# Products of probabilities and values in an attention kernel: one unbroken group per half pair, second head first

## Chip, cores and metric

The kernel runs on one core of one Trainium2 chip. The metric is the device time of one execution in microseconds (us); the time before the change is the median of three runs. The profile is of one further execution of the same program.

## What is computed

Two transformer blocks follow each other on 512 tokens of width 1024, all in 32-bit floats. The first block has an attention with 8 heads beside a convolution of 31 taps, and a feed-forward part; the second has a windowed attention with 16 query heads on 4 key heads ("GQA" below), then a latent attention with 16 heads ("MLA" below). The three attentions end in the same two steps, a softmax and the product of its probabilities with the values:

```python
def chunked_rel_attention(q, k, v, rel_bias):          # first block
    ...
    probs = jax.nn.softmax(scores, axis=-1).astype(v.dtype)
    out = jnp.einsum('bhcqk,bckhd->bcqhd', probs, vb)

def windowed_gqa(u, w_in, sink, w_out):                # GQA
    ...
        probs = jax.nn.softmax(jnp.concatenate([logits, sink_col], axis=-1), axis=-1)[..., :-1]
        return jnp.einsum('bkgqs,bskd->bqkgd', probs.astype(v_blk.dtype), v_blk)

def mla(u, w_in, q_norm, w_qb, kv_norm, w_kvb, w_out): # MLA
    ...
        probs = jax.nn.softmax(logits, axis=-1)
        return jnp.einsum('bhqs,bshd->bqhd', probs.astype(v.dtype), v)
```

A head has 64 columns of values in all three.

## The kernel before

Activations lie transposed: 128 features on the partitions, 512 tokens along the free dimension. A weight matrix comes in tiles of 128x1024 by DMA; ScalarE (ACT) copies a tile to a rounded form (`w_hi`, L83), VectorE (DVE) subtracts that from the tile (`w_lo`, L226), and each product with weights is three matmuls in float32r, high by high, high by low and low by high (`mm3`, L297 to L299). These are most of the work of TensorE (PE).

`attention` (from L537 on) is one generator for the three attentions; a `Spec` with the details of each is handed to it. It works on pairs of heads, 4 in the first block and 8 in each of the others. A pair has two halves of 256 queries (`hf`), a half has two blocks of 128 queries for each of the two heads, so four items. Per item:

- `scores`: a tile of scores in PSUM (`ps_s`; L837, L1266, L1610), softmax on DVE and ACT into a tile `P` in SBUF;
- `scale`, one step later: P is divided by its sum, on POOL (GpSimd) in GQA and MLA, on ACT in the first block (L556, L209, L212);
- `turn`, 3 or 4 steps later: P is turned by PE in pieces of 128x128 into `ps_pt` (L571, plain float32), and ACT copies the result into `PT` (L212), of which there are two buffers;
- `product`, two steps after the last turn of a half: for each block of 128 keys and each of the two heads one matmul of the head's 64 columns of values with the turned probabilities (L587, plain float32). The first head goes to partitions 0 to 63 of the PSUM tile `ps_o`, the second to partitions 64 to 127. A half has 8 such products in MLA, 6 in GQA, and 4 or 8 in the first block, 272 in all; the trace shows each as two matmul records, so 544. `ps_o` has one buffer for both halves of a pair; after the second half `Spec.out` reads it on DVE (and ACT) and frees it.

The attention alternates with a second generator that emits the weight matmuls of the same stage (`drive`). But the order in which the generators emit is not yet the order on the engines: a scheduler takes the emitted instructions, lets each engine take the ready one of the highest priority, by its own estimate of when operands are ready, and earlier emitted means higher priority. What comes out is a fixed list per engine, and on the chip each engine works through its list in order and waits where an operand is late. In the list of PE, the products of one half can therefore be broken up by turns, scores or weight matmuls. "Piece" below is a run of products with nothing else between them in that list.

Of the kernel before, what the change touches and what calls it, by code (L numbers as in the profile page):

```python
# [182 lines left out]
class Kernel:  # L183
# [353 lines left out]
    def attention(self, spec, pairs, ready, s):  # L537

        nc = self.nc
        items = [(p, hf, ii, hh) for p in range(pairs) for hf in range(2) for ii in range(2) for hh in range(2)]  # L540
        n = len(items)
        P, L, PT, O = {}, {}, {}, {}

        def scores(t):
            p, hf, ii, hh = items[t]
            i = 2 * hf + ii
            ps = self.ps("s")
            spec.qk(ps, p, hh, i)
            sb = s.tile([128, spec.width], F32, tag="P", name="P", bufs=spec.lag + 1)
            st = s.tile([128, 2], F32, tag="st", name="st", bufs=8)  # L550
            P[t] = spec.softmax(ps, sb, st, p, hh, i)
            L[t] = st

        def scale(t):
            st = L.pop(t)
            nc.vector.reciprocal(out=st[:, 0:1], in_=st[:, 1:2])  # L556
            if spec.scale_act:
                self.act(P[t], P[t], AF.Copy, scale=st[:, 0:1])
            else:
                self.ts(P[t], P[t], st[:, 0:1], 1.0, MUL, MUL, eng=nc.gpsimd)  # L560

        def turn(t):
            p, hf, ii, hh = items[t]
            i = 2 * hf + ii
            js = spec.keys(i)
            if (p, hf) not in PT:
                PT[p, hf] = s.tile([128, 2, spec.nj, 256], F32, tag="PT", name="PT", bufs=2)
            ps = self.ps("pt")
            x = P.pop(t)
            for a, j in enumerate(js):  # L570
                nc.tensor.transpose(ps[:, 128 * a:128 * a + 128], x[:, 128 * a:128 * a + 128], self.ident)  # L571
            j0 = js[0] - spec.first(hf)
            out = PT[p, hf][:, hh, j0:j0 + len(js), 128 * ii:128 * ii + 128]
            src = ps[:, :128 * len(js)].rearrange("p (a q) -> p a q", q=128)
            if spec.turn_act(t):
                self.act(out, src, AF.Copy)
            else:
                nc.vector.tensor_copy(out=out, in_=src)

        def product(p, hf):  # L580
            if hf == 0:
                O[p] = self.ps("o")
            pt = PT.pop((p, hf))
            js = spec.order(hf)
            for n_, (j, c0, c1) in enumerate(js):
                for hh in range(2):
                    nc.tensor.matmul(  # L587
                        out=O[p][64 * hh:64 * hh + 64, 256 * hf + c0:256 * hf + c1], lhsT=spec.v(p, hh, j),
                        rhs=pt[:, hh, j - spec.first(hf), c0:c1], start=(n_ == 0), stop=(n_ == len(js) - 1),
                        skip_group_check=True,  # L590
                    )
            if hf == 1:
                spec.out(p, O.pop(p))

        for t in range(n + spec.lag + 2):
            if t < n:
                while not ready(items[t][0]):
                    yield "wait"
                scores(t)
            if 0 <= t - 1 < n:  # L600
                scale(t - 1)
            yield
            late = t - spec.lag
            if 0 <= late < n:
                turn(late)
            if 0 <= late - 2 < n and items[late - 2][2:] == (1, 1):
                product(*items[late - 2][:2])
            yield
# [1126 lines left out]
```

## Time and profile before

| | |
|---|---|
| median of 3 runs | 1408.14 us (1407.62 to 1409.98) |
| the profiled execution | 1407.86 us, span of its instructions 1406.0 us |
| busy in the span | PE 1363.5 us (97%), DVE 898.7, ACT 684.4, POOL 268.3 |
| first block's attention and convolution | about 112 to 250 us of the span |
| GQA attention | about 820 to 985 us |
| MLA attention | about 1150 to 1313 us |

The profile names an instruction by line, engine, operation and tiles (`ps_o<-PT,V` is written from PT and V). A matmul's duration is the modelled time of one through the array; matmuls overlap, so what one costs is the distance from its start to the start of the next one. PEld is the load of a matmul's stationary operand, which can run beside another matmul. A "wait" is idle time of an engine, put down to the instruction that ended it.

### The profile page before, as it was taken

The numbers are of one execution on the slowest core, as the hardware profiler recorded it, in microseconds if no ns is written. First come the engines' busy times: TensorE is split into PE (matmuls) and PEld (weight loads), VectorE is DVE, ScalarE is ACT, GpSimd is POOL, SyncE is SP. The second block draws the span as 40 slices with busy tenths as digits, with TensorE's granted clock in tenths as the row PEclk, the third lists the DMA queues.
The fourth block names the chain that finished last, engine by engine and source line by source line (L and its number), as shares of the span: only waits on it lengthen the run. The fifth ranks groups of instructions, "written<-read, shape, count | busy, mean of one in ns | idle before, by whom it ended". The sixth has DMA issues, their size and how long they took to land.

```text
span 1406.0 us, 19239 instructions
## 1 busy us (share of the span) xinstructions
PE 1363.5 (97%) x6953; PEld 1078.5 (77%) x6953; DVE 898.7 (64%) x1560; ACT 684.4 (49%) x1222; POOL 268.3 (19%) x343
## 2 busy tenths in 40 slices
PE   6999999999899999999999999999999999999996
PEld 3887778788688888888887777777887876677785
DVE  6688999775777642355535555556586666665666
ACT  5247663434554432344424455656353467776543
POOL 0000001232201110011111134433123003332312
PEclk9999999999999999999999999999999999999998
DMA  8447626346425323323234442232233220111322
GB/s 338 149 134 200 191 90 217 98 152 238 152 86 166 115 72 98 120 91 105 70 95 158 128 129 84 79 90 76 87 124 110 90 87 22 46 38 38 109 94 68
DMA packets 55744, 162.99 MB, mean 116 GB/s; under 512 B 6753, under 2 KB 9185, under 8 KB 55650
## 3 DMA queue, kind: packets, MB, share of 16 engines
q1 hardware_dynamic: 55648, 161.76, 36.6%
q8 instruction: 55, 0.90, 0.3%
q14 instruction: 39, 0.32, 0.1%
q10 hardware_dynamic: 2, 0.00, 0.0%
HBM read 140.77 MB, written 6.29 MB: 105 GB/s over the span
## 4 chain that ended last, share of the span: by engine, by line
PE 85%; DVE 10%; ACT 2%; issue 2%; DMA 1%; SPq 0%; POOL 0%; DVEq 0%; ACTq 0%; POOLq 0%
PE ps_mm L297 21%; PE ps_mm L298 21%; PE ps_mm L299 21%; PE ps_o L587 5%; PE ps_pt L571 3%; PE ps_s L1610 3%; DVE w_lo L226 2%; PE ps_s L1266 2%; DVE conv L205 1%; PE ps_s L401 1%; DVE tA L202 1%; PE ps_pt L151 1%; PE ps_s L837 1%; ACT act_hi L212 1%; DVE act_lo L226 1%
## 5 line engine op out<-in xcount | busy, mean ns | idle before, releaser
L297 PE MATMUL ps_mm<-act_hi,w_hi 128*128 128x512 f32 (+1 forms) x1372 | 534.1, 391 | 5.1 <-ACT act_hi L212 3.9
L298 PE MATMUL ps_mm<-act_lo,w_hi 128*128 128x512 f32 (+1 forms) x1372 | 530.7, 387 | 1.7 <-DVE act_lo L205 1.6
L299 PE MATMUL ps_mm<-act_hi,w_lo 128*128 128x512 f32 (+1 forms) x1372 | 529.8, 387 | 2.1 <-DVE w_lo L226 2.1
L83 ACT ACTIVATE w_hi<-w_raw 128x1024 fp32r<-128x1024 f32 (+2 forms) x202 | 202.9, 1009 | 319.7 <-PE ps_mm L298 303.4
L226 DVE TENSOR_TENSOR w_lo<-w_raw,w_hi 128x1024 fp32r<-128x1024 f32 (+2 forms) x202 | 239.7, 1189 | 149.7 <-ACT w_hi L83 145.1
L297 PEld LDWEIGHTS ps_mm<-act_hi,w_hi 128*128 128x128 f32 x1372 | 258.8, 189 | 60.8 <-issue 5.4
L299 PEld LDWEIGHTS ps_mm<-act_hi,w_lo 128*128 128x128 f32 x1372 | 259.1, 189 | 55.5 <-DVE w_lo L226 3.2
L298 PEld LDWEIGHTS ps_mm<-act_lo,w_hi 128*128 128x128 f32 x1372 | 259.5, 189 | 53.2 <-DVE act_lo L205 2.1
L209 POOL TENSOR_SCALAR P<-P,st 128x512 f32<-128x512 f32 (+2 forms) x128 | 86.8, 680 | 175.2 <-DVE st L556 152.5
L212 ACT ACTIVATE PT<-ps_pt 128x512 f32<-128x512 f32 (+3 forms) x160 | 78.4, 497 | 32.6 <-PE ps_pt L571 31.1
L212 ACT ACTIVATE P<-P,st 128x385 f32<-128x385 f32 (+5 forms) x128 | 70.3, 557 | 49.1 <-DVE st L1279 38.7
L141 POOL TENSOR_TENSOR acc<-acc,sq 128x512 f32<-128x512 f32 x35 | 53.8, 1538 | 202.1 <-ACT sq L212 192.2
L205 DVE SCALAR_TENSOR_TENSOR conv<-u,vecs,conv 128x512 f32<-128x512 f32 x120 | 90.2, 758 | 1.0
L571 PE MATMUL ps_pt<-ident,P 128*128 128x128 f32 x496 | 83.2, 275 | 2.8 <-ACT P L212 1.7
L1066 POOL TENSOR_TENSOR val<-val,gate 128x512 f32<-128x512 f32 x22 | 28.9, 1315 | 289.3 <-ACT gate L212 289.3
L571 PEld LDWEIGHTS ps_pt<-ident,P 128*128 128x128 f32 x496 | 61.6, 140 | 25.3 <-POOL P L209 3.9
L587 PE MATMUL ps_o<-PT,V 128*64 128x256 f32 (+1 forms) x544 | 78.9, 372 | 0.5 <-ACT PT L212 0.2
L1615 DVE TENSOR_REDUCE st<-ps_s 128x1 f32<-128x512 f32 x64 | 44.0, 688 | 30.2 <-PE ps_s L1610 26.3
L1610 PE MATMUL ps_s<-Km,Qm 128*128 128x512 f32 x192 | 62.2, 425 | 0.0
L587 PEld LDWEIGHTS ps_o<-PT,V 128*64 128x64 f32 x544 | 39.0, 136 | 29.7 <-issue 15.2
L212 ACT ACTIVATE P<-ps_s,st 128x512 f32<-128x512 f32 x64 | 43.9, 686 | 20.6 <-DVE st L1615 17.1
L483 DVE CUSTOM_DVE_ANT_0 w_raw<-w_raw,c,vecs 128x1024 f32<-128x1024 f32 x32 | 44.5, 1389 | 12.9 <-DMA w_raw<-in_w_ada_dram 12.9
(254 smaller groups left out, 1643.9 us busy)
## 6 DMA issues: line engine op xcount, KB each, us to landing
w_raw<-in_w_up_dram SPq DMA_DIRECT2D x44, 512.0 KB, 3.4
w_raw<-in_w_in_dram SPq DMA_DIRECT2D x32, 512.0 KB, 4.3
w_raw<-in_w_ada_dram SPq DMA_DIRECT2D x32, 512.0 KB, 3.5
w_raw<-in_a_w_in_dram SPq DMA_DIRECT2D x18, 512.0 KB, 3.5
ada<-in_w_ada_dram SPq DMA_DIRECT2D x16, 512.0 KB, 7.1
w_raw<-in_ple_w_gate_dram SPq DMA_DIRECT2D x16, 512.0 KB, 3.3
w_raw<-in_b_w_in_dram SPq DMA_DIRECT2D x14, 512.0 KB, 3.4
Q<-stage SPq DMA_DIRECT2D x48, 128.0 KB, 2.4
```

Source lines behind the costliest of these rows:

```text
L83: k.nc.scalar.activation(out=hi, in_=src, func=AF.Copy)
L141: k.nc.gpsimd.tensor_tensor(out=self.sum, in0=self.sum, in1=x, op=ADD)
L205: return self.fix(self.nc.vector.scalar_tensor_tensor(out=out, in0=a, scalar=s, in1=b, op0=op0, op1=op1))
L209: return self.fix((eng or self.nc.vector).tensor_scalar(out=out, in0=a, scalar1=s1, scalar2=s2, op0=op0, **kw))
L212: return self.fix(self.nc.scalar.activation(out=out, in_=a, func=func, **kw))
L226: self.fix((eng or self.nc.vector).tensor_tensor(out=out, in0=x, in1=hi.bitcast(F32), op=SUB))
L297: mm(out=ps, lhsT=w[0], rhs=x[0], start=first, stop=False, **kw)
L298: mm(out=ps, lhsT=w[0], rhs=x[1], start=False, stop=False, **kw)
L299: mm(out=ps, lhsT=w[1], rhs=x[0], start=False, stop=last, **kw)
L571: nc.tensor.transpose(ps[:, 128 * a:128 * a + 128], x[:, 128 * a:128 * a + 128], self.ident)
L587: nc.tensor.matmul(out=O[p][64 * hh:64 * hh + 64, 256 * hf + c0:256 * hf + c1], lhsT=spec.v(p, hh, j), rhs=pt[:, hh, j - spec.first(hf), c ...
L1610: nc.tensor.matmul(out=ps, lhsT=Qb[p % 2][:, qa, hh, 128 * i:128 * i + 128], rhs=Kb[p % 2][:, ka, hh], start=(a == 0), stop=(a == 2))
```

## The change

The loop of the products stands inside a block of raised scheduling priority, and the two heads are emitted in the order second, first. Nothing else is changed; the same 272 products are computed.

```diff
             js = spec.order(hf)
-            for n_, (j, c0, c1) in enumerate(js):
-                for hh in range(2):
-                    nc.tensor.matmul(
...
+
+            with self.tc.high_priority():
+                for n_, (j, c0, c1) in enumerate(js):
+                    for hh in (1, 0):
+                        nc.tensor.matmul(
...
             if hf == 1:
                 spec.out(p, O.pop(p))
```

Every line of the kernel behind it has a number higher by two: L1610 becomes L1612, L1266 becomes L1268, the product L587 becomes L589.

The list of PE in MLA, where the second half of the second pair is computed, before (L571 turns, L587 products, L1610 scores, L297 and L298 weights; x8 is eight in a row):

```order
L571 MATMUL ps_pt<-ident,P 128x128
L587 MATMUL ps_o<-PT,V 64x256
L1610 MATMUL ps_s<-Km_8998,Qm_8996 128x512
L297 MATMUL ps_mm<-act_hi,w_hi 128x512
L587 MATMUL ps_o<-PT,V 64x256
L1610 MATMUL ps_s<-Km_8998,Qm_8996 128x512 x2
L587 MATMUL ps_o<-PT,V 64x256
L1610 MATMUL ps_s<-Km_8998,Qm_8996 128x512
L587 MATMUL ps_o<-PT,V 64x256 x2
L1610 MATMUL ps_s<-Km_8998,Qm_8996 128x512 x3
L587 MATMUL ps_o<-PT,V 64x256 x2
L571 MATMUL ps_pt<-ident,P 128x128
```

and with the change:

```order
L571 MATMUL ps_pt<-ident,P 128x128 x3
L1612 MATMUL ps_s<-Km_8998,Qm_8996 128x512
L571 MATMUL ps_pt<-ident,P 128x128 x3
L297 MATMUL ps_mm<-act_hi,w_hi 128x512
L1612 MATMUL ps_s<-Km_8998,Qm_8996 128x512 x2
L298 MATMUL ps_mm<-act_lo,w_hi 128x512
L589 MATMUL ps_o<-PT,V 64x256 x8
L1612 MATMUL ps_s<-Km_8998,Qm_8996 128x512 x4
```

The eight products stood in six pieces (the last, a single one, 14 matmuls further on) and stand in one now, four matmuls behind the last turn of their half.

The list of PE in GQA, where the second half of the second pair is computed, before (L1266 scores):

```order
L571 MATMUL ps_pt<-ident,P 128x128 x4
L587 MATMUL ps_o<-PT,V 64x256 x2
L1266 MATMUL ps_s<-Kg,Q 128x384 x2
L587 MATMUL ps_o<-PT,V 64x256
L1266 MATMUL ps_s<-Kg,Q 128x384 x2
L571 MATMUL ps_pt<-ident,P 128x128 x2
L587 MATMUL ps_o<-PT,V 64x256
L587 MATMUL ps_o<-PT,V 64x128 x2
L297 MATMUL ps_mm<-act_hi,w_hi 128x512
```

and with the change:

```order
L1268 MATMUL ps_s<-Kg,Q 128x384 x2
L298 MATMUL ps_mm<-act_lo,w_hi 128x512
L299 MATMUL ps_mm<-act_hi,w_lo 128x512
L297 MATMUL ps_mm<-act_hi,w_hi 128x512
L298 MATMUL ps_mm<-act_lo,w_hi 128x512
L571 MATMUL ps_pt<-ident,P 128x128 x2
L589 MATMUL ps_o<-PT,V 64x256 x4
L589 MATMUL ps_o<-PT,V 64x128 x2
L1268 MATMUL ps_s<-Kg,Q 128x384 x2
```

Three pieces became one, behind two turns that belong to the next half; the last turn of its own half lies 8 matmuls back.

Counted over the whole list, the products stand in 74 pieces before and in 40 now, one for each half: 14 and 8 in the first block, 25 and 16 in GQA, 35 and 16 in MLA. Of the 74, 42 hold an odd number of products (12, 10 and 20), in 4 of these the odd one being of 128 columns; of the 40 none does. At least 23 of the 40 stand five matmuls or fewer behind the last turn of their half. The list of the DMA queue is the same; on DVE, ACT and POOL neighbouring instructions change places.

## Rows read from the trace of the kernel before

**Rows 1.** Page, busy us (share of the span) and instructions of each engine.
```profile
PE 1363.5 (97%) x6953; PEld 1078.5 (77%) x6953; DVE 898.7 (64%) x1560; ACT 684.4 (49%) x1222; POOL 268.3 (19%) x343
```

**Rows 2.** Windows: length, then busy us of each engine, in the three attentions.
```profile
core 0: us, PE busy (x) PEld busy (x) DVE busy (x) ACT busy (x) POOL busy (x), PEclk, DMA share, GB/s
112.00:250.00 138.00, 134.45 (x678) 104.35 (x677) 129.17 (x255) 83.10 (x179) 8.19 (x10) 1.00 0.59 173
820.00:985.00 165.00, 164.41 (x902) 127.80 (x901) 98.03 (x256) 98.89 (x238) 67.16 (x138) 1.00 0.31 90
1150.00:1313.00 163.00, 161.58 (x890) 113.25 (x889) 101.60 (x198) 113.11 (x244) 52.23 (x67) 1.00 0.15 43
```

**Rows 3.** Waits of PE, whole span: us in total, times, longest.
```profile
PE ps_pt L151 <- DVE tA L202: 1.8, 1, 1.8
PE ps_pt L571 <- ACT P L212: 1.7, 1, 1.7
...
PE ps_o L587 <- ACT PT L212: 0.2, 1, 0.2
```

**Rows 4.** Timeline of PE in MLA: start us, duration, instructions merged.
```profile
1165.66 1.94 PE L587 MATMUL ps_o<-PT,V 128*64 128x256 f32 x14
1167.53 0.98 PE L1610 MATMUL ps_s<-Km,Qm 128*128 128x512 f32 x3
...
1172.84 1.95 PE L587 MATMUL ps_o<-PT,V 128*64 128x256 f32 x16
1174.72 0.97 PE L1610 MATMUL ps_s<-Km,Qm 128*128 128x512 f32 x3
...
1178.74 0.40 PE L299 MATMUL ps_mm<-act_hi,w_lo 128*128 128x512 f32 x1
1178.97 0.39 PE L297 MATMUL ps_mm<-act_hi,w_hi 128*128 128x512 f32 x1
...
1185.69 0.50 PE L1610 MATMUL ps_s<-Km,Qm 128*128 128x512 f32 x1
1186.03 0.40 PE L297 MATMUL ps_mm<-act_hi,w_hi 128*128 128x512 f32 x1
1186.36 0.65 PE L587 MATMUL ps_o<-PT,V 128*64 128x256 f32 x2
1186.93 0.73 PE L1610 MATMUL ps_s<-Km,Qm 128*128 128x512 f32 x2
...
1188.60 0.65 PE L587 MATMUL ps_o<-PT,V 128*64 128x256 f32 x4
1189.18 0.96 PE L1610 MATMUL ps_s<-Km,Qm 128*128 128x512 f32 x3
```

**Rows 5.** Timeline of PE in GQA: two unbroken groups, and what follows each.
```profile
860.97 1.30 PE L587 MATMUL ps_o<-PT,V 128*64 128x256 f32 x12
862.20 0.62 PE L1266 MATMUL ps_s<-Kg,Q 128*128 128x384 f32 x2
...
969.47 1.43 PE L587 MATMUL ps_o<-PT,V 128*64 128x256 f32 x12
970.83 0.50 PE L297 MATMUL ps_mm<-act_hi,w_hi 128*128 128x512 f32 x1
```

**Rows 6.** Tile PT: ACT's copies, ns shortest/median/longest.
```profile
L212 ACT ACTIVATE PT<-ps_pt x160: 257/492/605, 116.5 to 1306.2; 128x512 f32<-128x512 f32 x72, 128x256 f32<-128x256 f32 x40, 128x384 f32<-128x384 f32 x40, 128x128 f32<-128x128 f32 x8
```

**Rows 7.** Page, costliest groups: a turn on PE, and the exponential of MLA on ACT.
```profile
L571 PE MATMUL ps_pt<-ident,P 128*128 128x128 f32 x496 | 83.2, 275 | 2.8 <-ACT P L212 1.7
...
L212 ACT ACTIVATE P<-ps_s,st 128x512 f32<-128x512 f32 x64 | 43.9, 686 | 20.6 <-DVE st L1615 17.1
```

More of the change, by code (lines that the diff above doesn't have):

```diff
@@ L584, in product @@
             js = spec.order(hf)
-            for n_, (j, c0, c1) in enumerate(js):
-                for hh in range(2):
-                    nc.tensor.matmul(
[L588 to L591, printed above, removed]
+            with self.tc.high_priority():
+                for n_, (j, c0, c1) in enumerate(js):
+                    for hh in (1, 0):
+                        nc.tensor.matmul(
+                            out=O[p][64 * hh:64 * hh + 64, 256 * hf + c0:256 * hf + c1], lhsT=spec.v(p, hh, j),
+                            rhs=pt[:, hh, j - spec.first(hf), c0:c1], start=(n_ == 0), stop=(n_ == len(js) - 1),
+                            skip_group_check=True,
+                        )
             if hf == 1:
```

## The prediction

> **What bounds the kernel now.** I read the page first: PE is busy for 97% of the span, DVE for 64% and ACT for 49% [rows 1]. Then the windows of the three attentions, the only places that the change touches. In GQA and MLA PE works without a gap, 164.41 of 165 us and 161.58 of 163, while ACT and DVE are at 60 to 69% [rows 2]: there PE's own list sets the time. In the first block PE has 134.45 of 138 us but DVE also 129.17 [rows 2], and the longest wait of PE there is for DVE (`tA`, 1.8 us), at the end of the convolution [rows 3]: this stretch is bound by two engines. PE hardly waits for the products' operands: 0.2 us in all for a copy of PT [rows 3]. So the change can't remove waits. What it can remove is time in which PE is "busy" and gets little done, and the third view, the timeline of PE, shows that. All distances below are from start to start.
>
> **What a piece costs.** In MLA an unbroken group of 8 products (16 records) takes 1.88 us to the start of the scores behind it, a piece of 2 products 0.58 us [rows 4]. So 6 more products cost 1.30 us, 0.217 each, and a piece costs 0.58 - 0.43 = 0.15 us beyond its products. Its neighbours are stretched too: the weight matmul ahead of the piece at 1186.36 takes 0.33 us, and the single score matmul behind a piece at 1185.69 takes 0.34, where a float32r matmul among its like takes 0.23 [rows 4]. That adds 0.10 and 0.11: a piece costs 0.36 us.
>
> **What an odd piece costs.** A piece of one product takes 0.57 us, as much as a piece of two, and one of 7 takes 1.87, as much as 8 [rows 4]. Two products that follow each other for different heads share the array; the one without a partner costs its 0.217 us again (half that where it has 128 columns).
>
> The Trainium skill prices the first of these differently. "TensorEngine Tiling (Array Packing)", Key Properties, says that a change of tiling mode drains the engine, and "TensorE: Matmul & The Clock Gate", Part 2, gives a drain as about 128 cycles, an estimated 53 ns at 2.4 GHz, so 0.11 us for the way in and out. By that the term of the pieces would be 3.6 us, not 12.2. The rows show 0.36, and the measurement decides.
>
> **The sum on PE.** 34 pieces go (6, 9 and 19 in the three stretches): 34 x 0.36 = 12.2 us. 42 odd pieces go: 38 x 0.217 + 4 x 0.11 = 8.7. Together 20.9 us.
>
> **What the new place costs.** The groups now stand close behind their last turn, so their operands arrive at the last moment. The trace has such a case: the group of 6 in GQA that stands between weight matmuls takes 1.36 us, the same group behind turns 1.23 [rows 5]. I read the 0.13 as loads of the values that no longer run ahead of the products. Bounds: nothing, or all 40 groups; I take all, 40 x 0.13 = 5.2 us, since nearly every group gets this neighbourhood. That leaves 15.7 us on PE: 3.3 in the first block, 3.3 in GQA, 9.1 in MLA.
>
> **What waits come with it.** PE takes its list in order, so a group that waits for PT holds all scores and weight matmuls behind it. From the start of the last turn to PT it takes a turn (0.275 us) [rows 7] and a copy (0.492) [rows 6], with semaphores some 0.85 us as an estimate; three weight matmuls and the turn itself fill about that much, so 23 groups stand with no margin. If ACT is in an exponential (0.686 us) [rows 7] when the copy is due, PE waits for the rest of it, 0.34 us on average, in 65% of the cases by ACT's busy share [rows 2]: 23 x 0.65 x 0.34 = 5.1 us. The scheduler has its own estimate of ACT and has moved groups away where it saw this, so I take half, 2.5 us; the bounds are 0 and 5.1.
>
> In the first block PE's 3.3 us meet DVE, which has 8.8 us of slack in 138 [rows 2] and whose queue of convolution taps ends behind PE already [rows 3]. I let 2.0 us of the 3.3 go back into the wait for `tA`; bounds 0 and 3.3.
>
> **Edits at nothing.** Head order: both heads have the same number of columns, a piece starting with either runs at 0.217 per product in the same rows, and only partners matter. Evacuations of `ps_o` come at another time; the next pair's first product stands at least 14 matmuls (3.2 us) behind the group before it, and the cover is gone if DVE is more than 2 us late. DMA list: unchanged. Swaps on ACT, DVE and POOL: neighbours only, hidden by their idle third in GQA and MLA; in the first block they are in the 2.0.
>
> **Result.** 20.9 - 5.2 - 2.5 - 2.0 = 11.2 us. From the profiled execution, 1407.86 (span 1406.0 and 1.9 around it), that is 1396.7 us; the median of the runs is 0.3 higher, which I leave aside. Bounds: with no cost of the new place 1387.0; with all of them at their worst, 20.9 - 5.2 - 5.1 - 3.3 = 7.3, so 1400.6.
>
> **Rivals.**
>
> *Waits eat it and more (slower).* Every group meets an exponential that has just begun: 40 x 0.686 = 27.4 us against 15.7, so 1407.9 + 11.7 = 1419.6 us. It decides from a mean wait of 15.7/40 = 0.39 us per group on. For it: the groups have no margin, and a late group delays the scores that feed ACT. Against: the wait is 0.2 us now, ACT is idle for a third of the time, and a copy's delay of half an exponential needs an unlucky order in all 40 places.
>
> *Another engine sets the pace (no change).* If the chain of DVE, ACT and POOL behind the scores were just behind PE, faster products would only move the time into waits for P: about 1407.9. For it: PE waits for P on ACT once already (1.7 us) [rows 3], and the first block is such a place. Against: ACT 69%, DVE 62% and POOL 32% in MLA [rows 2].
>
> *Only the inside counts.* If the 0.10 and 0.11 of the neighbours are an overlap in modelled starts and not time, a piece costs 0.15: 34 x 0.15 + 8.7 - 5.2 - 2.5 - 2.0 = 4.1, so 1403.8. The skill's price of a drain, above, lies on this side. Against: the matmuls behind the stretched ones are later by just that amount.
>
> *The new place is free.* Loads run ahead and no copy is late: 1407.9 - 20.9 + 2.0 = 1389.0.
>
> That the pieces are not joined at all is excluded: the list shows 40.
>
> **Chances.** Forecast 0.74 (1390 to 1402 on its own), free place 0.09, only the inside 0.05, another engine 0.07, waits 0.05. 0.2%, 2.8 us, is about what a measurement of this kernel can tell from no change, so faster means below 1405.3: 0.73 of the forecast, 0.09, and 0.04 of the inside case, 0.86. Same: 0.01, 0.01 and 0.07, 0.09. Slower: 0.05. The range takes in the forecast's bounds, the free place and the inside case: 1389 to 1404.
>
> **What would show it.** In the changed profile: products (now L589) in 40 unbroken rows of x16, x12 or x8, the x16 at 1.9 to 2.0 us to the next start; the mean of a product record below the present one, since partnered records overlap; about 9 us less between the same weight tiles in MLA, 3 in GQA, 1 to 2 in the first block; a new wait of products for ACT's copy of PT of 1 to 5 us, and a longer wait for `tA` at the end of the convolution. The forecast is wrong if the x16 groups take over 2.2 us, if that new wait is over 6 us, or if PE is idle for P in MLA by more than a few us.

## The result, and the profile after

The changed kernel takes 1396.57 us, median of 5 runs (1394.39 to 1398.88), against 1408.14 (1407.51 to 1409.98) for the kernel before, run beside it: ratio 0.9916, 95% interval 0.9905 to 0.9928, so 11.6 us or 0.8% faster. Forecast were 1396.7 us and a range of 1389 to 1404. A second set of runs of the same program gave 1397.15 (ratio 0.9923, 0.9910 to 0.9936). The profiled execution took 1397.38 us, with a span of 1395.6.

The page after, busy times first, then the groups of scores and products and the products' loads (out<-in xcount | busy us, mean ns of one | idle before, releaser):

```profile
PE 1348.1 (97%) x6953; PEld 1071.5 (77%) x6953; DVE 895.9 (64%) x1560; ACT 681.4 (49%) x1222; POOL 266.0 (19%) x343
...
L1612 PE MATMUL ps_s<-Km,Qm 128*128 128x512 f32 x192 | 60.5, 421 | 2.5 <-DMA Qm<-act_hi 1.9
L589 PE MATMUL ps_o<-PT,V 128*64 128x256 f32 (+1 forms) x544 | 62.4, 368 | 0.3 <-ACT PT L212 0.2
L589 PEld LDWEIGHTS ps_o<-PT,V 128*64 128x64 f32 x544 | 35.5, 136 | 27.6 <-ACT PT L212 12.0
```

Against [rows 1] PE is busy for 15.4 us less, the span is 10.4 us shorter: some of the gain came back as idle time. The products are the same 544 records; their loads (PEld) wait 12.0 us for PT in 35 places (before 2.6 us in 6), the products themselves 0.2 as before.

Windows of the three attentions after, the stretches of [rows 2]:

```profile
112.00:250.00 138.00, 133.10 (x686) 104.00 (x685) 131.09 (x258) 83.08 (x179) 8.87 (x10) 1.00 0.60 177
820.00:985.00 165.00, 164.55 (x924) 128.97 (x923) 101.89 (x259) 99.27 (x239) 68.83 (x137) 1.00 0.32 93
1150.00:1313.00 163.00, 159.24 (x912) 115.52 (x913) 104.71 (x200) 114.53 (x246) 55.46 (x70) 1.00 0.17 50
```

GQA is still without a gap, and does more in its 165 us (924 PE records instead of 902). In MLA PE is now idle for 3.76 us of 163, it was 1.42 in [rows 2]. In the first block PE has 1.35 us less and DVE 1.9 us more.

Waits of PE after, whole span (us in total, times, longest):

```profile
PE ps_pt L151 <- DVE tA L202: 3.3, 1, 3.3
...
PE ps_s L1612 <- DMA Qm<-act_hi: 1.9, 3, 1.3
...
PE ps_mm L297 <- ACT ta L212: 1.4, 1, 1.4
...
PE ps_o L589 <- ACT PT L212: 0.2, 1, 0.2
```

The wait for `tA` grew from 1.8 [rows 3] to 3.3, as forecast. The new wait of the products for PT, forecast as 1 to 5 us, isn't there: 0.2 as before. Instead scores (L1612) wait in MLA; before, no wait of a score there (L1610) reached 0.2 us. The 1.7 us wait of a turn for P in [rows 3] is gone, and a weight matmul waits 1.4 us for ACT's `ta` in its stead.

Timeline of PE after, a group of 8 in MLA and one of 6 in GQA between weight matmuls, with what follows:

```profile
1158.93 1.95 PE L589 MATMUL ps_o<-PT,V 128*64 128x256 f32 x16
1160.81 0.51 PE L1612 MATMUL ps_s<-Km,Qm 128*128 128x512 f32 x1
```
```profile
843.12 0.40 PE L299 MATMUL ps_mm<-act_hi,w_lo 128*128 128x512 f32 x1
843.45 1.30 PE L589 MATMUL ps_o<-PT,V 128*64 128x256 f32 x12
844.68 0.50 PE L297 MATMUL ps_mm<-act_hi,w_hi 128*128 128x512 f32 x1
```

All 40 groups are unbroken. Those of 8 take the 1.88 us of [rows 4] (1.66 to 1.88, but for one of 3.10 in the first block whose successor L297 waits 1.4 us for ACT), all 16 groups of 6 take 1.23: the 1.36 of [rows 5] does not occur.

Where the time went is seen between the same weight matmuls in both traces. The first and last of the first block, of GQA and of MLA, before:

```profile
110.53 0.39 PE L297 MATMUL ps_mm<-act_hi,w_hi 128*128 128x512 f32 x1
...
279.26 0.39 PE L298 MATMUL ps_mm<-act_lo,w_hi 128*128 128x512 f32 x1
...
816.55 0.28 PE L386 MATMUL ps_s<-w_hi,act_hi 128*128 128x256 f32 x1
...
979.15 0.39 PE L297 MATMUL ps_mm<-act_hi,w_hi 128*128 128x512 f32 x1
...
1152.50 0.39 PE L297 MATMUL ps_mm<-act_hi,w_hi 128*128 128x512 f32 x1
...
1326.64 0.39 PE L297 MATMUL ps_mm<-o_hi,w_hi 128*128 128x512 f32 x1
```

and after:

```profile
110.50 0.39 PE L297 MATMUL ps_mm<-act_hi,w_hi 128*128 128x512 f32 x1
...
278.37 0.40 PE L298 MATMUL ps_mm<-act_lo,w_hi 128*128 128x512 f32 x1
...
815.92 0.28 PE L386 MATMUL ps_s<-w_hi,act_hi 128*128 128x256 f32 x1
...
973.34 0.39 PE L297 MATMUL ps_mm<-act_hi,w_hi 128*128 128x512 f32 x1
...
1146.97 0.39 PE L297 MATMUL ps_mm<-act_hi,w_hi 128*128 128x512 f32 x1
...
1316.18 0.39 PE L297 MATMUL ps_mm<-o_hi,w_hi 128*128 128x512 f32 x1
```

GQA: 162.60 before, 157.42 after, 5.2 us less (forecast 3.3). In the list after, one weight matmul of this stretch (0.23 us) stands behind its end, so the products gave 4.9 of the 5.2. MLA: 174.14 before, 169.21 after, 4.9 less (forecast 9.1). The first block: 168.73 before, 167.87 after, 0.9 less (forecast 1.3), of which 0.3 is lost again before GQA. So the total was as forecast and its parts were not. That is what the experiments are about.

### The profile page after: what moved, and what is told of

It is laid out like the page before. It is cut to its first block, busy times and chain, and to the rows that moved or that the text cites. A ratio compares the mean times of both kernels' runs of the same rounds, so it can differ in the third digit from the quotient of the medians.

```text
span 1395.6 us, 19255 instructions
## 1 busy us (share of the span) xinstructions
PE 1348.1 (97%) x6953; PEld 1071.5 (77%) x6953; DVE 895.9 (64%) x1560; ACT 681.4 (49%) x1222; POOL 266.0 (19%) x343
## 4 chain that ended last, share of the span: by engine, by line
PE 85%; DVE 9%; ACT 2%; issue 2%; DMA 1%; POOL 1%; SPq 0%; DVEq 0%; ACTq 0%; POOLq 0%
PE ps_mm L297 22%; PE ps_mm L298 21%; PE ps_mm L299 21%; PE ps_o L589 4%; PE ps_pt L571 4%; PE ps_s L1612 3%; DVE w_lo L226 2%; PE ps_s L1268 1%; DVE conv L205 1%; PE ps_s L401 1%; PE ps_s L839 1%; PE ps_pt L151 1%; ACT act_hi L212 1%; DMA ada<-in_w_ada_dram 1%; DVE tA L202 0%
## 5 line engine op out<-in xcount | busy, mean ns | idle before, releaser
L297 PE MATMUL ps_mm<-act_hi,w_hi 128*128 128x512 f32 (+1 forms) x1372 | 535.7, 392 | 6.9 <-ACT act_hi L212 4.0
L298 PE MATMUL ps_mm<-act_lo,w_hi 128*128 128x512 f32 (+1 forms) x1372 | 531.9, 388 | 1.7 <-DVE act_lo L205 1.6
L299 PE MATMUL ps_mm<-act_hi,w_lo 128*128 128x512 f32 (+1 forms) x1372 | 530.5, 387 | 2.5 <-DVE w_lo L226 2.5
L297 PEld LDWEIGHTS ps_mm<-act_hi,w_hi 128*128 128x128 f32 x1372 | 258.7, 189 | 60.6 <-issue 5.3
L299 PEld LDWEIGHTS ps_mm<-act_hi,w_lo 128*128 128x128 f32 x1372 | 259.0, 189 | 55.5 <-DVE w_lo L226 3.8
L298 PEld LDWEIGHTS ps_mm<-act_lo,w_hi 128*128 128x128 f32 x1372 | 259.6, 189 | 51.8 <-DVE act_lo L205 2.1
L209 POOL TENSOR_SCALAR P<-P,st 128x512 f32<-128x512 f32 (+2 forms) x128 | 83.7, 659 | 166.8 <-DVE st L556 158.8
L571 PE MATMUL ps_pt<-ident,P 128*128 128x128 f32 x496 | 82.2, 275 | 1.4 <-POOL P L209 0.9
L571 PEld LDWEIGHTS ps_pt<-ident,P 128*128 128x128 f32 x496 | 61.2, 140 | 23.3 <-issue 2.8
L1612 PE MATMUL ps_s<-Km,Qm 128*128 128x512 f32 x192 | 60.5, 421 | 2.5 <-DMA Qm<-act_hi 1.9
L589 PE MATMUL ps_o<-PT,V 128*64 128x256 f32 (+1 forms) x544 | 62.4, 368 | 0.3 <-ACT PT L212 0.2
L589 PEld LDWEIGHTS ps_o<-PT,V 128*64 128x64 f32 x544 | 35.5, 136 | 27.6 <-ACT PT L212 12.0
L483 DVE CUSTOM_DVE_ANT_0 w_raw<-w_raw,c,vecs 128x1024 f32<-128x1024 f32 x32 | 44.0, 1373 | 12.4 <-DMA w_raw<-in_w_ada_dram 12.4
L1617 DVE TENSOR_REDUCE st<-ps_s 128x1 f32<-128x512 f32 x64 | 43.6, 687 | 11.6 <-PE ps_s L1612 10.6
L212 ACT ACTIVATE sq<-x 128x512 f32<-128x512 f32 (+1 forms) x62 | 34.3, 560 | 30.9 <-DVE x L202 21.7
```

Of the source, the lines that this page charges most:

```text
L209: return self.fix((eng or self.nc.vector).tensor_scalar(out=out, in0=a, scalar1=s1, scalar2=s2, op0=op0, **kw))
L212: return self.fix(self.nc.scalar.activation(out=out, in_=a, func=func, **kw))
L297: mm(out=ps, lhsT=w[0], rhs=x[0], start=first, stop=False, **kw)
L298: mm(out=ps, lhsT=w[0], rhs=x[1], start=False, stop=False, **kw)
L299: mm(out=ps, lhsT=w[1], rhs=x[0], start=False, stop=last, **kw)
L589: nc.tensor.matmul(out=O[p][64 * hh:64 * hh + 64, 256 * hf + c0:256 * hf + c1], lhsT=spec.v(p, hh, j), rhs=pt[:, hh, j - spec.first(hf), c ...
```

## The experiments

"Stretch" below is the time between these same weight matmuls. The table gives, for each kernel, the pieces of products and the odd ones among them in GQA and MLA, the length of the stretch against the kernel before, and what the two prices of the prediction (0.36 us a piece, 0.217 an odd one; 0.11 for the two narrow ones at a raise of 60, elsewhere narrow ones are counted in full) make of the difference. Each measured length is that of one profiled execution.

| kernel | us, median | GQA pieces/odd | GQA by prices | GQA measured | MLA pieces/odd | MLA by prices | MLA measured |
|---|---|---|---|---|---|---|---|
| before | 1408.14 | 25/10 | | | 35/20 | | |
| changed | 1396.57 | 16/0 | -5.4 | -5.2 | 16/0 | -11.2 | -4.9 |
| changed, again | 1397.15 | 16/0 | -5.4 | -5.3 | 16/0 | -11.2 | -3.0 |
| priority, first head first | 1418.64 | 27/22 | +3.3 | +2.8 | 32/32 | +1.5 | +3.3 |
| second head first, no priority | 1402.18 | 24/8 | -0.8 | -0.6 | 28/6 | -5.6 | -4.6 |
| priority in GQA alone | 1397.30 | 16/0 | -5.4 | -5.3 | 28/6 | -5.6 | -4.6 |
| priority in MLA alone | 1401.19 | 24/8 | -0.8 | -0.6 | 16/0 | -11.2 | -4.7 |
| priority raised by 60 | 1399.02 | 21/6 | -2.5 | -2.8 | 16/0 | -11.2 | -6.5 |
| priority raised by 20 | 1428.83 | 47/34 | +13.1 | +11.0 | 45/26 | +4.9 | +7.4 |

The column of GQA follows the prices to within 0.5 us, and to within 2 at a raise of 20 (about 1 if the nine narrow lone products there are priced at 0.11). In the five rows that show -5.2, -5.3, -2.8 and +11.0, one weight matmul stands behind the end of the stretch, 0.2 us of the difference. The column of MLA follows the prices to within 1 to 3 us, except where the list has 16 pieces: there 5 to 8 us of 11 are missing, in four kernels (-4.9, -3.0, -4.7, -6.5).

These four have the same list of PE in MLA, and the traces show why they differ. In three of them some transfers of `Qm`, which a score needs, land late: in the changed kernel up to 3.5 us after their issue, where about 1.9 is usual. The score behind them waits 1.26 us:

```profile
1219.66 0.70 PE L1612 MATMUL ps_s<-Km,Qm 128*128 128x512 f32 x2 [1.26 <-DMA Qm<-act_hi]
...
DMA to landing us min/median/max: 1.9/2.0/3.5
```

The same score waits 1.57 us in the second profile of the changed kernel and 1.61 with priority in MLA alone, where transfers take up to 3.8 us. The profile puts these two waits down to ACT, but in all three the score starts 0.13 to 0.14 us after the slowest transfer has landed. With the raise of 60 the same transfers are in time, and that wait is not there:

```profile
DMA to landing us min/median/max: 1.9/1.9/2.0
```

In the second profile of the changed kernel, moreover, the granted clock is 0.50 (1.2 GHz, the lower of its two levels) in a window of 3.3 us that begins 0.5 us after the end of that wait, and the group of 8 there takes 3.21 us instead of 1.88 (window with the columns of [rows 2], then the group):

```profile
1218.20:1221.50 3.30, 3.30 (x16) 1.54 (x16) 0.00 (x0) 0.00 (x0) 0.47 (x1) 0.50 0.22 55
...
1218.82 3.27 PE L589 MATMUL ps_o<-PT,V 128*64 128x256 f32 x16
```

Half the clock for 3.3 us is an estimated 1.65 us. Without the late transfers and without the slow clock the four stretches would be 6.2 to 6.5 us shorter than before, as an estimate; the one profile that has neither shows -6.5. Why the transfers were late is not known.

What is left of the difference to -11.2 shows when each stretch of MLA is divided: the distances behind products, those behind all other matmuls, both without idle time, and the idle time (us, summed from the starts in the traces).

| kernel | stretch | products | other matmuls | idle |
|---|---|---|---|---|
| before | 174.1 | 37.1 | 135.6 | 1.4 |
| second head first, no priority | 169.5 | 33.1 | 135.5 | 0.9 |
| priority in MLA alone | 169.4 | 30.0 | 135.1 | 4.3 |
| changed | 169.2 | 30.0 | 135.3 | 3.9 |
| priority raised by 60 | 167.6 | 30.0 | 134.9 | 2.6 |

The products give 7.1 us, what the prices say for their inside (19 x 0.15 + 20 x 0.217 = 7.2). The other matmuls should give the neighbours' share, 19 x 0.21 = 4.0, and give 0.3 to 0.7. The rest is idle time, 1.2 to 2.9 us more than before.

**Priority alone.** The changed kernel with the heads in the old order:

```diff
-                    for hh in (1, 0):
+                    for hh in (0, 1):
```

> Raised priority as in the change, but the first head emitted first, as before. Theory A (the gain is the number of pieces and of odd pieces in PE's list, whatever brings them about): this list has 73 pieces, 66 of them odd, so with the first head first the priority joins nothing, since the last copy of a half is always the second head's and the first head's products leave early and alone. By 0.36 us a piece and 0.217 us an odd piece against before (74 and 42): 1408 + 24 x 0.217 - 0.4 = about 1413 us, slower than before. Theory B (the raised priority is what counts, the order of the heads is nothing, as the prediction had it): 1396.6, as the change.

Measured: 1418.64 us (1418.13 to 1419.66), ratio 1.0080 (1.0065 to 1.0095): slower than before, 22 us slower than the changed kernel. The list has 73 pieces, 66 of them odd. Timeline of PE in MLA, one half of a pair:

```profile
1168.10 0.27 PE L571 MATMUL ps_pt<-ident,P 128*128 128x128 f32 x1
1168.30 0.65 PE L589 MATMUL ps_o<-PT,V 128*64 128x256 f32 x2
1168.88 0.55 PE L571 MATMUL ps_pt<-ident,P 128*128 128x128 f32 x3
...
1170.73 1.94 PE L589 MATMUL ps_o<-PT,V 128*64 128x256 f32 x14
1172.60 0.73 PE L1612 MATMUL ps_s<-Km,Qm 128*128 128x512 f32 x2
```

The turns of the second head come last in a half. With the first head first, its first product is ready one copy earlier, and with raised priority it leaves at once, alone (x2 records); the seven others follow as a second piece. Every half of 8 in MLA breaks up as 1 and 7. So priority makes unbroken groups only if the product emitted first is also the one that becomes ready last. The edit that the prediction costed at nothing decides the sign. The total is 5.6 us above theory A's 1413: GQA is as the prices say, but MLA is 1.8 us longer than they say, and the first block about 3 us longer at an unchanged 14 pieces and 12 odd ones. That part stays unexplained.

**Head order alone.** The loop of before, without priority:

```diff
-            with self.tc.high_priority():
-                for n_, (j, c0, c1) in enumerate(js):
-                    for hh in (1, 0):
+            for n_, (j, c0, c1) in enumerate(js):
+                for hh in (1, 0):
```

> Second head first, but no raised priority. Theory A: the list has 61 pieces, 14 of them odd, so 13 x 0.36 + 28 x 0.217 = 10.8 us less on PE than before; with the loss to DVE in the first block and to waits in MLA seen in the change (about a half of what the list promises there) 1399 to 1402 us, so most of the gain of the change. Theory B (the priority is what counts): 1408.

Measured: 1402.18 us (1399.37 to 1403.52), ratio 0.9960 (0.9945 to 0.9974). This is just above theory A's 1399 to 1402, and about half of the gain, most of it in MLA (-4.6 us), where the odd pieces fall from 20 to 6.

**Products by head.** Still one group per half, but all products of one head, then all of the other:

```diff
-                for n_, (j, c0, c1) in enumerate(js):
-                    for hh in (1, 0):
+                for hh in (1, 0):
+                    for n_, (j, c0, c1) in enumerate(js):
```

> As the change, but inside a group all products of the second head come first, then all of the first; pieces, their places and every other instruction's place are as in the change. Theory A (two products that follow each other share the array when they belong to different heads): only the pair at the change of heads shares, so a group of 8 takes 1.88 + 3 x 0.433 = 3.2 us, one of 6 in GQA about 0.87 more, and the 40 groups 42 us more on PE; with some of it covered by DVE in the first block 1430 to 1439 us. Theory B (odd pieces cost more for another reason, the change of tile size alone has a price): within 0.2% of 1396.6.

Measured: 1419.48 us (1418.77 to 1421.03), ratio 1.0087 (1.0072 to 1.0102). Timeline of PE in MLA:

```profile
1171.36 2.86 PE L589 MATMUL ps_o<-PT,V 128*64 128x256 f32 x16
1174.15 0.50 PE L1612 MATMUL ps_s<-Km,Qm 128*128 128x512 f32 x1
```

The same 8 products in one piece take 2.79 us instead of 1.88. The pieces are the same 40, so this is the price of neighbours that don't alternate between the heads, and it is a large one. That products of different heads share the array is one reading of it; that a product costs more behind one that adds to the same place in PSUM is another, and no run tells the two apart. The size, 0.91 us for a group of 8, is less than the 1.3 expected, and the total is below the 1430 to 1439 of theory A.

**A third bank for the scores of MLA.** Every third tile of scores there takes its PSUM from the pool of the weight matmuls:

```diff
-            ps = self.ps("s")
+            ps = self.ps("mm" if spec.scale_act is False and spec.nj == 4 and t % 3 == 2 else "s")
```

> As the change, but in MLA every third tile of scores lies in one of the three PSUM buffers of the weight matmuls instead of the two of the scores. In the changed kernel's trace MLA gives back some 6 us of what the list promises, in waits of the score matmuls. Theory A1 (they wait for ACT's exponential to free one of the two score buffers): about 2 to 4 us faster than the change, 1393 to 1395. Theory A2 (they wait for Qm by DMA and for other things, or the wait only moves on to the weight matmuls, whose buffers are now shared): 1396 to 1398.

Measured: 1395.97 us (1394.66 to 1396.83), ratio 0.9918 (0.9903 to 0.9932): the same as the changed kernel (0.9916 and 0.9923). MLA's stretch is 6.6 us shorter than before, as much as with the raise of 60; in this profile, too, the transfers behind that wait are in time. Lending the scores a bank of the weight matmuls gives nothing more. What a third bank of their own would give was not tried.

**Priority in one attention alone.** The second head is first everywhere; priority is raised in GQA only, or in MLA only:

```diff
-            with self.tc.high_priority():
+            with (self.tc.high_priority() if spec.nj == 3 else ExitStack()):
```
```diff
-            with self.tc.high_priority():
+            with (self.tc.high_priority() if spec.width == T and pairs == 8 else ExitStack()):
```

> Second head first in all three attentions; raised priority in GQA alone. The list has 53 pieces, 6 of them odd (changed kernel: 40 and 0; second head first alone: 61 and 14). Theory S (by stages: priority pays in GQA, about 4.6 us beyond the head order by the two traces, and next to nothing in MLA and the first block): second head first alone was 1402.2, so about 1397.6, and MLA's stretch stays as far below the one before as with head order alone (4.6 us). Theory P (each piece 0.36 us and each odd one 0.217 us, wherever it stands): 13 x 0.36 + 6 x 0.217 = 6.0 us over the changed kernel, about 1402.6.

> Second head first in all three attentions; raised priority in MLA alone. 49 pieces, 8 odd. Theory S: the same as second head first alone, about 1402, since priority in MLA only trades pieces for waits of the scores. Theory P: 9 x 0.36 + 8 x 0.217 = 5.0 us over the changed kernel, 1401.6, with MLA's stretch 12 x 0.36 + 6 x 0.217 = 5.6 us shorter than with second head first alone. The total hardly tells the two apart; the MLA stretch does (no gain over head order alone, or some 5 us).

Measured: in GQA alone 1397.30 us (1396.88 to 1397.79), ratio 0.9921 (0.9906 to 0.9935), as much as with priority in all three; in MLA alone 1401.19 (1400.30 to 1403.56), ratio 0.9950 (0.9937 to 0.9963), no more than head order alone can give within the intervals. Theory S held in both numbers, theory P fell in MLA: 12 pieces and 6 odd ones went there, and the stretch stayed (-4.7 after -4.6). Without the wait behind the late transfers it would be an estimated -6.3, still far from the -10.2 of theory P.

Windows from 1146 to 1300 us show where they went (columns as in [rows 2]). Second head first without priority:

```profile
1146.00:1300.00 154.00, 153.07 (x865) 109.13 (x864) 98.49 (x194) 111.59 (x242) 52.59 (x67) 1.00 0.14 42
```

and with priority in MLA alone:

```profile
1146.00:1300.00 154.00, 149.72 (x865) 108.24 (x864) 98.21 (x194) 111.24 (x243) 51.68 (x67) 1.00 0.15 41
```

Both do the same number of PE records in 154 us; the second is idle for 4.28 us, the first for 0.93. By starts over the whole stretch, products take 33.1 and 30.0 us, turns 28.1 and 27.1, scores 49.8 and 48.8, and the distances behind the 240 weight matmuls 58.5 and 63.5: what the joined products give, PE loses behind weight matmuls, in front of scores (16 such distances with 4.9 us, then 20 with 8.7) and of products (1 with 0.3, then 8 with 2.8). The page puts the longest wait of a score, the 1.6 us behind the late transfers, down to ACT; head order alone, then priority in MLA:

```profile
L1610 PE MATMUL ps_s<-Km,Qm 128*128 128x512 f32 x192 | 61.9, 423 | 0.3 <-DMA Qm<-act_lo 0.2
```
```profile
L1612 PE MATMUL ps_s<-Km,Qm 128*128 128x512 f32 x192 | 60.5, 421 | 2.8 <-ACT P L212 1.6
```

**The price of a piece by itself.** A smaller raise of the priority:

```diff
-            with self.tc.high_priority():
+            with self.tc.high_priority(60):
```

> The changed kernel with a smaller raise of priority (60): the lists of PE are alike but for one group of 6 in MLA, which is now 6 pieces of one product each, between weight matmuls. It measures the price of a piece by itself. Price with neighbours (0.36 a piece, 0.217 an odd 256 column product, 0.11 an odd 128 column one): 5 x 0.36 + 4 x 0.217 + 2 x 0.11 = 2.9 us more between the same weight tiles around this group, total about 1399.5. Price of the inside alone (0.15 a piece): 0.75 + 1.09 = 1.8 us more, about 1398.4.

Measured: 1399.02 us (1398.08 to 1399.95), ratio 0.9933 (0.9918 to 0.9947). The group that is broken up is the first of GQA, not one of MLA as the expectation says. Timeline of PE in this kernel:

```profile
825.80 0.39 PE L299 MATMUL ps_mm<-act_hi,w_lo 128*128 128x512 f32 x1
826.03 0.39 PE L297 MATMUL ps_mm<-act_hi,w_hi 128*128 128x512 f32 x1
826.34 0.65 PE L589 MATMUL ps_o<-PT,V 128*64 128x256 f32 x2
826.92 0.49 PE L298 MATMUL ps_mm<-act_lo,w_hi 128*128 128x512 f32 x1
827.35 0.65 PE L589 MATMUL ps_o<-PT,V 128*64 128x256 f32 x2
827.92 0.49 PE L299 MATMUL ps_mm<-act_hi,w_lo 128*128 128x512 f32 x1
...
831.13 0.43 PE L589 MATMUL ps_o<-PT,V 128*64 128x128 f32 x2
831.49 0.50 PE L297 MATMUL ps_mm<-act_hi,w_hi 128*128 128x512 f32 x1
...
833.44 0.40 PE L299 MATMUL ps_mm<-act_hi,w_lo 128*128 128x512 f32 x1
```

and of the same place in the changed kernel:

```profile
825.89 0.39 PE L299 MATMUL ps_mm<-act_hi,w_lo 128*128 128x512 f32 x1
826.21 1.30 PE L589 MATMUL ps_o<-PT,V 128*64 128x256 f32 x12
827.44 0.50 PE L297 MATMUL ps_mm<-act_hi,w_hi 128*128 128x512 f32 x1
...
830.76 0.39 PE L299 MATMUL ps_mm<-act_hi,w_lo 128*128 128x512 f32 x1
```

Between the same two L299, with 6 products and 14 weight matmuls, lie 7.64 and 4.87 us: five more pieces and six lone products cost 2.77 us. With the neighbours' 0.21 the forecast price gives 2.9, without it 1.8. Between weight matmuls the stretched neighbours are real time. By the drain of about 128 cycles that the Trainium skill states ("TensorE: Matmul & The Clock Gate", Part 2), an estimated 0.11 us a piece for the way in and out, it would be 0.55 + 1.09 = 1.6 us. The measurement decides: if the six lone products cost their 1.09, a piece costs 0.34.

**The most pieces.** The raise is only 20:

```diff
-            with self.tc.high_priority():
+            with self.tc.high_priority(20):
```

> The changed kernel with a raise of priority of only 20: second head still first, but 105 pieces, 66 of them odd, the most of any version here. With 0.36 us a piece and 0.217 an odd one: 65 x 0.36 + 66 x 0.217 = 37.7 us over the changed kernel, about 1434. With 0.15 a piece, if the stretched neighbours are no real time: 24.1 us, about 1421. If pieces are mostly hidden by waits that PE would have had anyway: below 1412.

Measured: 1428.83 us (1427.75 to 1430.10), ratio 1.0145 (1.0129 to 1.0160). The total lies between the two prices, 32.3 us over the changed kernel for 37.7 and 24.1. In GQA 31 pieces and 34 odd ones more cost 16.2 us (by the full price about 17.6, with the nine narrow ones at 0.11; by the inside alone about 11.1). In MLA they cost 12.4 us where the full price says 16.1; that is most of what is missing from the total.

**Groups a step later, and more weight matmuls between the attention's steps in MLA.** Two edits of the changed kernel, the first one apart, the second apart, then both:

```diff
-        for t in range(n + spec.lag + 2):
+        for t in range(n + spec.lag + 3):
...
-            if 0 <= late - 2 < n and items[late - 2][2:] == (1, 1):
-                product(*items[late - 2][:2])
+            if 0 <= late - 3 < n and items[late - 3][2:] == (1, 1):
+                product(*items[late - 3][:2])
```
```diff
-        self.project(main(), self.attention(Spec, 8, lambda p: p in ready, pa), 0.5, O, heads, outer, 1)
+        self.project(main(), self.attention(Spec, 8, lambda p: p in ready, pa), 0.7, O, heads, outer, 1)
```

> The changed kernel with each group of products emitted one score tile later (all three attentions), still at raised priority, 40 pieces, none odd. If groups that stand close behind their last turn cost time (the 5.2 us for the new place and the 2.5 us of waits for PT in my sum), up to 7.7 us come back: about 1389. If that place costs nothing, as the trace of the changed kernel reads (0.2 us of waits of products for PT), nothing comes back: 1395 to 1398.

> The changed kernel with one number of MLA changed: 0.7 instead of 0.5 steps of weight matmuls per step of attention, so that scores, turns and products stand further apart among weight matmuls (the list still has 40 pieces, none odd). Theory W (MLA gave back some 6 us because its scores now wait for ACT's exponentials and for Qm where attention stands dense): with 40% more weight matmuls between them most of these waits go, 3 to 5 us less than the changed kernel, 1392 to 1394. Rival (the waits are not from the density; or what is gained there is lost where attention ends later than the weight matmuls that should cover it): within 1.5 us of the changed kernel, 1395 to 1398, or above.

> Both last edits on the changed kernel: products one score tile later and 0.7 steps of weight matmuls per step of attention in MLA; 40 pieces, none odd. If what each seemed to give in its own call is real (1.8 and 1.0 us against the changed kernel's 1396.57) and they add, about 1393.8; if these were scatter of the runs, 1395 to 1398, the same as the changed kernel run beside it here.

> The changed kernel once more, unedited, so that the version before it in this call is compared with it on one chip and against the same runs of the kernel before: 1396 to 1398, and the same stretches as in its first profile to within 1 us, but for the waits for Qm's transfer in MLA, 2.3 us there, which I expect to differ by a microsecond or two from run to run.

Measured: a step later 1395.57 us (1394.52 to 1396.19), ratio 0.9907 (0.9890 to 0.9924); 0.7 instead of 0.5 1394.78 (1392.13 to 1396.23), ratio 0.9900 (0.9883 to 0.9918); both 1395.97 (1395.48 to 1396.22), ratio 0.9912 (0.9898 to 0.9926), beside 1397.15 (1396.60 to 1399.15) for the changed kernel. The place close behind the last turn costs nothing like the 7.7 us of the sum: a step later brings 1.0 and 1.6 us against the two medians of the changed kernel, which is not clear of the noise. The 0.7 came out between the two theories, 0.8 us above the upper end of W's; together with the later groups only 0.6 and 1.2 us are left against the two medians, so it is not a gain that can be relied on. Theory W is not decided by this: in the profile with both edits the score behind late transfers waits 1.33 us again, in that of the 0.7 alone 0.36. None of the three is shown to beat the changed kernel: the intervals overlap. The unedited kernel's second profile has MLA 1.9 us longer than its first, where at most 1 us was expected; the lower clock, an estimated 1.65 us, accounts for most of that.

## Why the prediction was right, and where it was not

**Right: the mechanism and the price inside a group.** The products are joined to 40 unbroken groups at 1.88 and 1.23 us. The price of a missing partner is confirmed by the halves that break up as 1 and 7 (0.58 + 1.87 instead of 1.88 us, so 0.57 more where the prices say 0.58), the whole price of a piece between weight matmuls by the group that was broken up (2.77 us measured, 2.9 by the prices). GQA's stretch follows the sum of the prices in every kernel of the table, though with the change its products give more than their share (4.1 us for 3.5) and the other matmuls less (0.7 for 1.9). The rival that counted only the inside of a piece is out between weight matmuls, and so is the rival of waits at every group.

**Wrong: the new place, 5.2 us.** The groups show nothing of it. The group of 6 at 1.36 us [rows 5] was no sign of its place: with the change all 16 take 1.23, those between weight matmuls too (843.45 above). This is why GQA gained some 5 us instead of 3.3.

**Wrong: waits of the products for PT, 2.5 us.** They are 0.2. Only their loads wait longer for PT than before, 12.0 us in 35 places, and hardly any of it reaches the products.

**Wrong: MLA, 9.1 us.** Two steps failed. The first is the term of the neighbours, 0.10 + 0.11 us a piece, read from single weight and score matmuls and then taken for all pieces. In MLA, where most pieces stand between turns and scores, its 4.0 us came to 0.3 to 0.7: the other matmuls take 135.6 us with 35 pieces and 134.9 to 135.3 with 16. Whether the pieces there stretch their neighbours less, or the new order stretches other matmuls instead, is open. The second is that PE's own list sets the time in MLA since it had 161.58 of 163 us [rows 2]. With head order alone that still held (0.9 us idle). With priority added PE is idle for 2.6 to 4.3 us; in the profiles with 3.9 and more, 1.3 to 1.6 of that is the wait behind late transfers of `Qm`. This is the rival "another engine sets the pace", given 0.07, come true for a small part. No engine is full there (ACT 114.53 and DVE 104.71 of 163 us); what the rest of the idle time waits for was not settled.

**Wrong: head order at nothing.** The prediction looked at the cost of a product alone. But the order decides which product is ready last, and with it whether the scheduler can send one off alone. Priority without it is 0.8% slower than before.

**Nearly right in the first block.** 1.3 us were forecast, 0.9 measured, with the longer wait for `tA` (1.5 us more, 2.0 forecast) and the new wait of 1.4 us for ACT's `ta` in place of the 1.7 for P.

**The total** was right because the errors cancelled: 5.2 + 2.5 us of costs that did not come, against some 8 us that the prices promised and that did not arrive, 6.3 of them in MLA. That they cancelled was luck; only half of the reasons held.

## What to carry to other kernels

Where a scheduler may break up a group of small matmuls, count the pieces in TensorE's list and those without a partner, and price both from the timeline by distances from start to start. Price the neighbours for each kind of neighbour that the pieces have: here what was read between weight matmuls held there and not among turns and scores. A raised priority joins a group only if its first instruction is the one whose operand comes last; otherwise it sends that one off alone and makes it worse. And "the engine has no gap" says what bounds a stretch now, not how far: take the cheaper half of a change first and look whether the other half still buys anything (here priority in GQA alone gives as much as in all three). Before a difference between two profiles is explained by the edit, look at the granted clock and at the landing of the transfers in both.

## What was not expected of the hardware

A product of 64 columns that stands alone between weight matmuls takes 0.58 us to the next start and, with what it does to its neighbours, stretches the distance between weight matmuls from 0.23 to 1.00 us (826.92 to 827.92 in the broken group, with the product of 827.35 between them). In one group of alternating heads the same product costs 0.217 us. Eight without alternation take 2.79 us, more than eight alternating (1.88) and less than the 3.2 expected if only the pair at the change of heads shares its time; why was not pursued.
